# Turning the rows ahead of the FFN by products with a diagonal of the norm's factors, in a two-layer encoder trunk

## The chip, the cores and the metric

The kernel runs on one core of a Trainium2 chip. The metric is the device time of one execution in microseconds; the median of three runs of the kernel before is 2181.53 us (2178.12 to 2184.14). Everything is computed in float32: a product of full accuracy is made either of three products of operands rounded to a shorter type (`fp32r`: high by high, high by low, low by high) or, in a few places, of one plain float32 product.

## The reference, cut to what matters

Two layers work on x of 1024 tokens by 1024 features. Layer 0 mixes by attention, layer 1 by a gated linear recurrence; each ends with a SwiGLU FFN. Every sub-layer is wrapped in two norms:

```python
def rmsnorm(x, g):
    xf = x.astype(jnp.float32)
    y = xf * lax.rsqrt(jnp.mean(xf * xf, axis=-1, keepdims=True) + RMS_EPS)
    return (y * g.astype(jnp.float32)).astype(x.dtype)

# per layer
x = x + rmsnorm(m, norm_mix_post[layer])          # m: the mixer's output
h = rmsnorm(x, norm_ffn_pre[layer])
f = swiglu(h, ffn_w_gate[layer], ffn_w_up[layer], ffn_w_down[layer])
x = x + rmsnorm(f, norm_ffn_post[layer])
```

The change concerns the norm `rmsnorm(x, norm_ffn_pre)`. Its gain vector is multiplied into the FFN's weights, so what is left to do on the rows is the factor per token, 1/sqrt(mean square + eps).

## The kernel before, in words

**Where it happens.** `out_product` computes the mixer's output product (1024 x 1024 by 1024 x 1024) in three passes over the eight token tiles of 128: tiles 0, 1, 2, then 3, 4, 5, then 6 and 7. The product of a tile lands in PSUM (`ps`), and from there it goes through a chain that is the same for every tile t:

1. `rstd`: ScalarE squares `ps` and sums the rows (L179), GpSimd adds eps and takes the power -1/2 (L183, L184).
2. VectorE multiplies `ps` with the gain of the post norm into `mg` (L251), then adds the old x: `x = mg * rs + x` (L257). A DMA stores x (L259).
3. `pre_norm`: `rstd` again, on x (L179, L183, L184), with `mg` as a place for the squares that nobody reads. ScalarE then writes the scaled rows x * rs into `mg` (L213).
4. `turn`: TensorE turns the eight 128 x 128 blocks of `mg` with transposes against the identity (L223) into two PSUM banks `pst`.
5. `HiddenS.take`: ScalarE copies the two banks back into `mg` (L85), VectorE forms differences `tf` (L89) for a Strassen product, ScalarE rounds the pieces into `hS` (L96) and VectorE forms the remainders (L89, also into `hS`).

`hS` is the moving operand of the FFN's gate and up products (`strassen`, L759 to L761).

**What sets the order.** A scheduler with its own estimates of durations puts the instructions of each engine into one fixed list; every engine then works through its list in order, waiting on semaphores. Some orders are written by hand with `behind`: the turns of tiles 3, 4 and 5 stand between the plain float32 products of tile 6 (`raw` by `act`, L602), and the turn of tile 6 stands behind the first of the seven FFN products that use the first 256 columns of `hS` (tiles 0 to 3). The weights of the FFN's first block are prepared in the same stretch (`gate_load`: L717, L729, L730, L736 to L743).

**Buffers.** `mg` has 3, `pst` has 2 banks (tag `tr`), and a turn fills both. x has 2 buffers (tag `nx`), except for tiles 2 and 5, which use a place of their own; the loads of x for tiles 3, 4, 6 and 7 therefore wait until an earlier tile's x is no longer read.

The same stretch occurs twice, at 438 to 600 us (layer 0) and at 1430 to 1570 us (layer 1) of the profiled span. `pre_norm` is also used behind the first FFN (`HiddenT`, 8 tiles, 64 transposes); the change leaves that use as it is.

Of the kernel before, what the change touches and what calls it, by code (L numbers as in the profile page):

```python
# [11 lines left out]
AF = mybir.ActivationFunctionType  # L12
# [3 lines left out]
P = 128  # L16
# [83 lines left out]
class Trunk:  # L100
# [106 lines left out]
    def pre_norm(self, pool, x, h, g, sink, t, psum, later=False):  # L207


        nc = self.nc  # L210
        rs = self.rstd(pool, [x], h)
        if g is None:
            self.scaled = nc.scalar.activation(h, x, AF.Copy, scale=rs).ins  # L213
        else:
            self.scaled = nc.vector.scalar_tensor_tensor(h, x, rs, g, op0=ALU.mult, op1=ALU.mult).ins

        def turn():
            pst = []
            for q in range(2):
                ps = psum()  # L220
                for j in range(4):
                    kt = 4 * q + j
                    self.turned[t] = nc.tensor.transpose(  # L223
                        ps[:, j * P:(j + 1) * P], h[:, kt * P:(kt + 1) * P], self.ident).ins
                pst.append(ps.rearrange("p (a b) -> p a b", a=4))
            return lambda: sink.take(t, pst, h, pool)

        if later:
            return turn
        turn()()  # L230
# [342 lines left out]
    def psum(self):  # L573
        return self.pp.tile([P, 512], F32, tag="mm", bufs=6, name=self.uid("ps"))
# [712 lines left out]
```

## Time and profile before

| | |
|---|---|
| median of 3 runs | 2181.53 us (2178.12 to 2184.14) |
| the profiled execution, its own time | 2188.6 us |
| its span, first to last instruction | 2186.8 us |
| TensorE busy | 2158.0 us, 99% of the span |
| VectorE, ScalarE, GpSimd busy | 1500.0, 1173.2, 220.4 us |
| mean granted TensorE clock | 0.996 |

In the profile, PE is TensorE's matmul side and PEld its loading of stationary operands; DVE is VectorE, ACT ScalarE, POOL GpSimd, SP the queue that issues most DMAs. A row of the timeline gives the start, the time until the result is written (matmuls overlap, so the distance from one start to the next is what one costs), engine, line, operation, tiles and, in brackets, the idle time ahead of it and what ended it. Rows of equal instructions that follow each other are merged. A row of the groups gives the total busy time, the mean of one in ns, and the idle time just ahead of them. A row of the windows gives the busy time of each engine in a stretch and the mean clock that TensorE was granted there (1.00 is full speed).

### The profile page before, as it was taken

What the parts mean: (1) busy time and instruction counts of PE and PEld (TensorE: products, weight loads), DVE (VectorE), ACT (ScalarE), POOL (GpSimd) and SP (SyncE); (2) the same over time, 40 slices, a digit from 0 to 9 for tenths busy, and PEclk for the clock granted to TensorE, in tenths of its full rate; (3) what the DMA queues carried; (4) which work ended last, traced back from release to release, by engine and by line L of the source; (5) the groups of instructions that cost most, each with busy time, mean ns of one, the idle gap of its engine ahead of it and who ended that gap; (6) DMA issues with size and microseconds to landing.
All of it is one profiled execution on the core that took longest, in us unless ns stands there. A gap on an engine that the chain in (4) does not pass through costs nothing.

```text
span 2186.8 us, 30432 instructions
## 1 busy us (share of the span) xinstructions
PE 2158.0 (99%) x11140; PEld 1803.8 (82%) x11140; DVE 1500.0 (69%) x2458; ACT 1173.2 (54%) x2174; POOL 220.4 (10%) x398
## 2 busy tenths in 40 slices
PE   9999999999999999999999999999999999999998
PEld 8888989878788888888887777887788888888886
DVE  5747555656877677767778667437786767758675
ACT  7656555556755445433446576537755454424452
POOL 2111113121100000000002333102100000000011
PEclk9999999999999999999999999999999999999999
DMA  7111012126334233336467311356133333328565
GB/s 284 44 49 49 30 40 64 43 99 205 133 103 133 92 118 99 106 106 242 136 196 225 98 49 54 95 199 230 63 130 102 121 97 98 110 87 293 169 183 154
DMA packets 167453, 269.42 MB, mean 123 GB/s; under 512 B 13964, under 2 KB 94860, under 8 KB 167304
## 3 DMA queue, kind: packets, MB, share of 16 engines
q1 hardware_dynamic: 166520, 265.38, 37.9%
q10 hardware_dynamic: 784, 2.10, 0.3%
q8 instruction: 87, 1.43, 0.3%
q14 instruction: 62, 0.51, 0.1%
HBM read 199.80 MB, written 65.54 MB: 121 GB/s over the span
## 4 chain that ended last, share of the span: by engine, by line
PE 86%; DVE 5%; ACT 3%; DMA 2%; issue 2%; POOL 1%; SPq 0%; POOLq 0%; DVEq 0%; ACTq 0%
PE ps L760 13%; PE ps L759 13%; PE ps L761 13%; PE ps L602 6%; PE ps L845 5%; PE ps L846 5%; PE ps L844 5%; PE pso L370 3%; PE tr L435 3%; PE psq L167 3%; PE psq L168 2%; PE psq L169 2%; PE ps L168 2%; PE ps L169 2%; PE ps L167 2%
## 5 line engine op out<-in xcount | busy, mean ns | idle before, releaser
L759 PE MATMUL ps<-hS,q 128*128 128x512 f32 (+1 forms) x1288 | 490.4, 381 | 0.0
L760 PE MATMUL ps<-hS,q 128*128 128x512 f32 (+1 forms) x1288 | 489.9, 381 | 0.5 <-DVE hS L89 0.5
L761 PE MATMUL ps<-hS,q 128*128 128x512 f32 (+1 forms) x1288 | 489.2, 380 | 0.0
L730 DVE TENSOR_TENSOR q<-raw,q 128x512 fp32r<-128x512 f32 x308 | 205.6, 688 | 180.7 <-ACT q L729 180.1
L760 PEld LDWEIGHTS ps<-hS,q 128*128 128x128 f32 x1288 | 243.1, 189 | 47.0 <-DVE hS L89 0.9
L761 PEld LDWEIGHTS ps<-hS,q 128*128 128x128 f32 x1288 | 243.0, 189 | 46.1
L759 PEld LDWEIGHTS ps<-hS,q 128*128 128x128 f32 x1288 | 242.7, 189 | 46.1 <-DVE tf L89 0.2
L729 ACT CAST q<-raw 128x512 fp32r<-128x512 f32 x308 | 178.8, 619 | 165.4 <-DVE raw L738 127.6
L845 PE MATMUL ps<-o,o 128*128 128x512 f32 x616 | 240.2, 390 | 0.5 <-DVE o L840 0.4
L846 PE MATMUL ps<-o,o 128*128 128x512 f32 x616 | 237.7, 389 | 0.0
L717 ACT ACTIVATE raw<-raw,gcol 128x256 f32<-128x256 f32 x352 | 150.8, 502 | 138.7 <-DMA raw<-in_ffn_w_up_dram 74.8
L844 PE MATMUL ps<-o,o 128*128 128x512 f32 x616 | 218.6, 390 | 1.8 <-ACT o L839 1.8
L839 ACT CAST o<-raw 128x512 fp32r<-128x512 f32 x173 | 104.2, 622 | 148.3 <-PE ps L846 52.5
L183 POOL TENSOR_SCALAR rs<-ss 128x1 f32<-128x1 f32 x52 | 34.0, 654 | 1416.2 <-ACT junk L179 1344.1
L840 DVE TENSOR_TENSOR o<-raw,o 128x512 fp32r<-128x512 f32 x173 | 116.1, 688 | 53.1 <-ACT o L839 52.6
L844 PEld LDWEIGHTS ps<-o,o 128*128 128x128 f32 x616 | 115.3, 188 | 27.2 <-ACT o L839 3.7
L845 PEld LDWEIGHTS ps<-o,o 128*128 128x128 f32 x616 | 115.6, 188 | 25.6 <-DVE o L840 1.8
L846 PEld LDWEIGHTS ps<-o,o 128*128 128x128 f32 x616 | 115.6, 188 | 24.0
L157 DVE TENSOR_TENSOR wlo<-raw,whi 128x1024 fp32r<-128x1024 f32 x76 | 93.4, 1229 | 58.6 <-ACT whi L156 57.3
L423 DVE TENSOR_TENSOR_SCAN pr<-pr,zero 128x128 f32<-128x128 f32 (+7 forms) x64 | 86.6, 1359 | 51.3 <-POOL pr L420 49.6
L156 ACT CAST whi<-raw 128x1024 fp32r<-128x1024 f32 x76 | 79.8, 1052 | 52.1 <-PE ps L168 23.4
L167 PE MATMUL psq<-hT,whi 128*128 128x512 f32 x256 | 102.4, 400 | 1.2 <-ACT v L310 1.0
(208 smaller groups left out, 4278.6 us busy)
## 6 DMA issues: line engine op xcount, KB each, us to landing
raw<-in_ffn_w_gate_dram SPq DMA_DIRECT2D x44, 512.0 KB, 4.2
raw<-in_ffn_w_up_dram SPq DMA_DIRECT2D x44, 512.0 KB, 4.2
gS<-c SPq DMA_DIRECT2D x88, 256.0 KB, 3.8
raw<-gS SPq DMA_DIRECT2D x88, 256.0 KB, 2.8
gA<-c SPq DMA_DIRECT2D x66, 256.0 KB, 3.4
raw<-gA SPq DMA_DIRECT2D x44, 256.0 KB, 2.7
t<-in_ffn_w_down_dram SPq DMA_DIRECT2D x22, 512.0 KB, 6.5
raw<-in_ffn_w_down_dram SPq DMA_DIRECT2D x41, 256.0 KB, 4.8
```

What stands on the lines that cost most here:

```text
L167: nc.tensor.matmul(ps, wh[:, kt, cols], hh[:, kt, :], start=kt == 0, stop=False)
L602: self.matmul = nc.tensor.matmul(ps[:, n * 512:(n + 1) * 512], x, y[:, n, :], start=first and i == 0, stop=last and i == len(passes) - 1).ins
L717: nc.scalar.activation(raw[:, i], raw[:, i], AF.Copy, scale=gain[:, 4 * k + i:4 * k + i + 1])
L729: self.last = nc.scalar.copy(t[:, 0], src).ins
L730: self.last_lo = nc.vector.tensor_tensor(t[:, 1], src, t[:, 0].bitcast(F32), op=ALU.subtract).ins
L759: nc.tensor.matmul(ps, a[:, 0, kt, :], bh, start=kt == 0, stop=False)
L760: nc.tensor.matmul(ps, a[:, 0, kt, :], bl, start=False, stop=False)
L761: self.matmul = nc.tensor.matmul(ps, a[:, 1, kt, :], bh, start=False, stop=kt == 3).ins
L840: tt(t[:, 1], src, t[:, 0].bitcast(F32), op=ALU.subtract)
L844: nc.tensor.matmul(ps, a[0], b[:, 0], start=first, stop=False)
L845: nc.tensor.matmul(ps, a[0], b[:, 1], start=False, stop=False)
L846: self.matmul = nc.tensor.matmul(ps, a[1], b[:, 0], start=False, stop=last).ins
```

## The change

Where the receiver is `HiddenS` (the norms ahead of both FFNs, 16 tiles in all), `pre_norm` no longer writes the scaled rows. ScalarE writes a 128 x 128 diagonal matrix instead: the identity, each row scaled with that token's factor, into a part of `mg`. Step 4 is then no transpose of scaled rows but a plain float32 product of x's block (stationary) with that diagonal (moving), which turns the block and scales it at once. Steps 1, 2, 3's squares, and 5 stay.

```diff
         rs = self.rstd(pool, [x], h)
-        if g is None:
+        scaling = isinstance(sink, HiddenS)
+        if scaling:
+            diag = h[:, 512:512 + P]
+            self.scaled = nc.scalar.activation(diag, self.ident, AF.Copy, scale=rs).ins
+        elif g is None:
             self.scaled = nc.scalar.activation(h, x, AF.Copy, scale=rs).ins
...
                 for j in range(4):
                     kt = 4 * q + j
-                    self.turned[t] = nc.tensor.transpose(
-                        ps[:, j * P:(j + 1) * P], h[:, kt * P:(kt + 1) * P], self.ident).ins
+                    o, c = ps[:, j * P:(j + 1) * P], slice(kt * P, (kt + 1) * P)
+                    self.turned[t] = (nc.tensor.matmul(o, x[:, c], diag, start=True, stop=True) if scaling else
+                                      nc.tensor.transpose(o, h[:, c], self.ident)).ins
```

The scheduler's lists change with it. In the changed kernel the lines behind the edit stand 4 or 5 further down: L213 is L215 (the diagonal), L223 is L228, L251 is L256, L257 is L262, L602 is L607, L612 is L617; L85, L89, L96, L156 and L179 keep their numbers. In the rows below a buffer's number belongs to the built program: `ps_5878`, `ps_5879`, `ps_5880` are the products of tiles 3, 4 and 5 of layer 0, and `pst_5806` with `pst_5811` the two banks of tile 0's turn.

TensorE in layer 0, in the second pass, around the turn of tile 0. Before:

```order
L602 MATMUL ps_5879<-whi_5947,al_5944 128x512
L602 MATMUL ps_5880<-whi_5887,ah_5883 128x512
...
L602 MATMUL ps_5880<-whi_5917,al_5914 128x512
L602 MATMUL ps_5880<-whi_5947,ah_5943 128x512
L223 MATMUL pst_5806<-ident,mg_5768 128x128 x4
L223 MATMUL pst_5811<-ident,mg_5768 128x128 x4
L602 MATMUL ps_5880<-wlo_5948,ah_5943 128x512
```

and now:

```order
L607 MATMUL ps_5879<-whi_5947,al_5944 128x512
L228 MATMUL pst_5806<-mg_5768,x_5769 128x128 x4
L228 MATMUL pst_5811<-mg_5768,x_5769 128x128 x4
L607 MATMUL ps_5880<-whi_5887,ah_5883 128x512
L607 MATMUL ps_5880<-wlo_5888,ah_5883 128x512
L607 MATMUL ps_5880<-whi_5887,al_5884 128x512
```

Tile 0's turn stands 13 products of tile 5 further ahead; the turns of tiles 1 and 2 move ahead likewise, to about where those of tiles 0 and 1 stood.

ScalarE in layer 0, after tile 1's x has been squared (`mg_5778,ss_5832`). `ah_5973`, `whi_6007`, `ah_6003`, `whi_6037` are the rounded operands of the next steps of the second pass. Before:

```order
L213 ACTIVATE mg_5768<-x_5769,rs_5790 128x1024
L213 ACTIVATE mg_5778<-x_5779,rs_5831 128x1024
L179 ACTIVATE mg_5796,ss_5863<-x_5797 128x1024
L612 CAST ah_5973<-act_5971 128x384
L156 CAST whi_6007<-raw_6005 128x1024
L213 ACTIVATE mg_5796<-x_5797,rs_5862 128x1024
L612 CAST ah_6003<-act_6001 128x384
L156 CAST whi_6037<-raw_6035 128x1024
L85 COPY mg_5768<-pst_5806 128x512
L85 COPY mg_5768<-pst_5811 128x512
```

and now:

```order
L215 ACTIVATE mg_5768<-ident,rs_5790 128x128
L215 ACTIVATE mg_5778<-ident,rs_5831 128x128
L179 ACTIVATE mg_5796,ss_5863<-x_5797 128x1024
L85 COPY mg_5768<-pst_5806 128x512
L215 ACTIVATE mg_5796<-ident,rs_5862 128x128
L85 COPY mg_5768<-pst_5811 128x512
L96 CAST hS_5513<-mg_5768 128x8x64
L96 CAST hS_5515<-mg_5768 128x4x64
L617 CAST ah_5973<-act_5971 128x384
L156 CAST whi_6007<-raw_6005 128x1024
```

The copies of tile 0's turned banks, and two roundings behind them, now stand ahead of the operands `ah_5973` and `whi_6007`.

VectorE in layer 0, where tile 6's product `ps_6257` becomes `mg_6355` and then `x_6356` (`tf_6215` belongs to tile 4, `tf_6246` to tile 5, `q` and `raw` to the FFN's weights). Before:

```order
L89 TENSOR_TENSOR tf_6215<-tf_6215,mg_6131 128x256
L251 TENSOR_TENSOR mg_6355<-ps_6257,g_5766 128x1024
L89 TENSOR_TENSOR hS_5518<-tf_6215,hS_5517 128x16x64
L257 SCALAR_TENSOR_TENSOR x_6356<-mg_6355,rs_6359,x_6356 128x1024
L743 TENSOR_TENSOR raw_6387<-raw_6387,raw_6381 128x4x128
```

and now:

```order
L89 TENSOR_TENSOR tf_6215<-tf_6215,mg_6131 128x256
L89 TENSOR_TENSOR hS_5518<-tf_6215,hS_5517 128x16x64
L256 TENSOR_TENSOR mg_6355<-ps_6257,g_5766 128x1024
L89 TENSOR_TENSOR tf_6246<-mg_6162 128x256 x2
L262 SCALAR_TENSOR_TENSOR x_6356<-mg_6355,rs_6359,x_6356 128x1024
L735 TENSOR_TENSOR q_6397<-raw_6381,q_6397 128x512
```

Tile 4's 1024-wide remainder stands ahead of `mg_6355` instead of behind it, and two 256-wide differences of tile 5 stand between `mg_6355` and `x_6356`. Layer 1 has the same three moves. On the SP queue the loads of x for tiles 4 and 5 stand a few issues further back and the store of tile 5's x stands ahead of the loads for tiles 6 and 7; GpSimd's list is the same.

## The prediction

> **What bounds the kernel now.** I read the page's busy times and its chain first.
>
> ```profile
> PE 2158.0 (99%) x11140; PEld 1803.8 (82%) x11140; DVE 1500.0 (69%) x2458; ACT 1173.2 (54%) x2174; POOL 220.4 (10%) x398
> PE 86%; DVE 5%; ACT 3%; DMA 2%; issue 2%; POOL 1%; SPq 0%; POOLq 0%; DVEq 0%; ACTq 0%
> ```
>
> TensorE is busy for 99% of the span and carries 86% of the chain that ended last: work added to it is paid in full, unless it falls into one of its few waits; work taken from ScalarE is worth only what TensorE waits for ScalarE. So the next views are the stretch around the changed norms (layer 0's, as windows) and TensorE's own waits.
>
> ```profile
> 482.00:520.00 38.00, 38.00 (x176) 31.16 (x173) 20.79 (x21) 19.96 (x30) 6.14 (x10) 1.00 0.63 205
> ...
> 545.00:573.00 28.00, 28.00 (x110) 18.14 (x109) 27.31 (x45) 24.84 (x46) 7.24 (x13) 1.00 0.55 202
> 573.00:580.00 7.00, 4.84 (x28) 4.63 (x28) 5.15 (x7) 5.56 (x9) 2.94 (x4) 0.76 0.70 225
> ```
> ```profile
> engine line waited for: us in total, times, longest us
> PE pst L223 <- ACT mg L213: 5.0, 2, 2.8
> PE pst L223 <- ACT mg L85: 1.8, 1, 1.8
> ```
>
> In each window the first pair is PE's busy time. In the first two it has no gap at all; VectorE joins it from 545 on (27.31 of 28.00). Only at 573 to 580 does TensorE stand still (4.84 of 7.00), with the clock down (0.76). In both layers together TensorE waits 5.0 us for the scaled rows, twice, and 1.8 us for the copies of a turned bank, once. That, and what the waits do to the clock, is all that a faster scaling could win.
>
> **The change part by part. First, what a turn costs TensorE.**
>
> ```profile
> L435 PE MATMUL tr<-ident,pr 128*128 128x128 f32 x528 | 83.2, 278 | 0.1
> ...
> L370 PE MATMUL pso<-pt,v 128*64 128x128 f32 x1056 | 66.6, 276 | 1.5 <-ACT pt L441 1.4
> ...
> L602 PE MATMUL ps<-raw,act 128*128 128x512 f32 x64 | 28.5, 592 | 0.0
> ...
> L223 PE MATMUL pst<-ident,mg 128*128 128x128 f32 x128 | 18.7, 290 | 6.8 <-ACT mg L213 5.0 <-ACT mg L85 1.8
> ```
>
> Count the records. A transpose leaves one (L223: 16 tiles x 8 = 128). A plain float32 product leaves two: `raw` by `act` is 2 tiles x 4 steps x 2 halves x 2 layers = 32 products and 64 records, and attention's L370 has 1056 for the 528 blocks that L435 turns one by one. So each of the 128 changed turns becomes two passes. What one costs is the distance between starts:
>
> ```profile
> 520.96 0.39 PE L602 MATMUL ps<-whi,ah 128*128 128x512 f32 x1
> 521.19 1.03 PE L223 MATMUL pst<-ident,mg 128*128 128x128 f32 x8
> 521.98 0.48 PE L602 MATMUL ps<-wlo,ah 128*128 128x512 f32 x1
> 522.29 0.40 PE L602 MATMUL ps<-whi,al 128*128 128x512 f32 x1
> ...
> 557.23 1.88 PE L602 MATMUL ps<-raw,act 128*128 128x512 f32 x4
> 558.95 1.04 PE L223 MATMUL pst<-ident,mg 128*128 128x128 f32 x8
> ```
>
> Eight transposes and the next product take 522.29 - 521.19 = 1.10 us; less the product's 0.23 (520.96 to 521.19) that is 0.87, or 0.109 each. A float32 pass of 512 columns takes (558.95 - 557.23)/4 = 0.43, so 0.108 for 128 columns. Both say 0.109 per pass, 0.218 per product, +0.87 us per tile, and over 16 tiles **+13.9 us**. Bounds for the price of a pass: L370's passes follow at 0.058 (40 in 2.33 us of the chain below), but use half the columns of the array, so that two of them may overlap; at 0.058 the change adds 16 x (16 x 0.058 - 0.87) = +0.9 us. If a pass could not hide its own weight load it would take 0.108 + 0.14 and the change add 49 us; both full-size rows hide it. I take 0.109, the row of the same shape.
>
> ```profile
> 85.11 2.33 PE pso L370 x40
> ```
> ```profile
> L223 PEld LDWEIGHTS pst<-ident,mg 128*128 128x128 f32 x128 | 15.8, 148 | 11.3 <-ACT mg L213 5.4 <-ACT mg L85 3.4 <-issue 1.1
> ```
>
> The Trainium skill's page "TensorE: Matmul & The Clock Gate", Terms, calls the transpose mode four times faster for FP32. By that rule a product costs 4 x 0.109 and the change adds 16 x 8 x 3 x 0.109 = 41.8 us; the two records of each plain product speak for two times, not four.
>
> **Second, ScalarE.** A 128 x 1024 scaling becomes a 128 x 128 one:
>
> ```profile
> L213 ACT ACTIVATE mg<-x,rs 128x1024 f32<-128x1024 f32 x16 | 18.4, 1152 | 10.4 <-POOL rs L184 10.2
> ...
> L415 ACT ACTIVATE pr<-pr,mn 128x128 f32<-128x128 f32 x8 | 3.2, 398 | 2.0 <-DVE mn L407 2.0
> ```
>
> 1.15 us falls to about 0.40 (L415, from SBUF to SBUF and of the same shape), so each tile is ready 0.75 us earlier. For 13 of 16 tiles nobody waits and this is worth nothing. The other three:
>
> ```profile
> 576.47 1.97 PE L223 MATMUL pst<-ident,mg 128*128 128x128 f32 x8 [2.16 <-ACT mg L213]
> ...
> 579.91 0.28 PE L761 MATMUL ps<-hS,q 128*128 128x256 f32 x1
> 580.03 0.28 PE L759 MATMUL ps<-hS,q 128*128 128x256 f32 x1
> ...
> 1526.94 1.14 PE L223 MATMUL pst<-ident,mg 128*128 128x128 f32 x8 [1.77 <-ACT mg L85]
> ...
> 1545.47 1.69 PE L223 MATMUL pst<-ident,mg 128*128 128x128 f32 x8 [2.83 <-ACT mg L213]
> ...
> 1549.40 0.28 PE L759 MATMUL ps<-hS,q 128*128 128x256 f32 x1
> ```
>
> Tile 4 of layer 1 waits 1.77 us for the copies of tile 3's bank, which stand behind tile 4's scaling on ScalarE. They come 0.75 earlier, and TensorE, with tile 3's turn doubled, arrives 0.87 later: 1.77 - 0.75 - 0.87 leaves 0.15. **-1.6 us.**
>
> Tile 6 waits 2.16 and 2.83 us. The doubled turns of tiles 3 to 5 don't shorten this by themselves, since tile 6's product stands behind them too and starts the chain later. The scaling gives 0.75. VectorE's new order gives a little more: a 1.22 us remainder stood between `mg` and x, now two 256-wide differences stand there.
>
> ```profile
> 568.34 1.22 DVE L89 TENSOR_TENSOR hS<-tf,hS 128x1024 fp32r<-128x1024 f32 x1
> ...
> 571.87 0.76 DVE L89 TENSOR_TENSOR tf<-mg 128x256 f32<-128x256 f32 x2
> ...
> 574.42 1.22 DVE L251 TENSOR_TENSOR mg<-ps,g 128x1024 f32<-128x1024 f32 x1
> ```
>
> That is 1.22 - 0.76 = 0.46 at most, none if the remainder now delays `mg` by as much; I take 0.35. Bounds for each wait: a gain of 0.4 to all of it. **-2.2 us** for both; 1.05 and 1.7 us of waiting stay.
>
> The clock is the third thing that a shorter wait moves.
>
> ```profile
> 577.00:578.00 1.00, 1.00 (x6) 1.00 (x5) 0.86 (x2) 0.94 (x2) 0.00 (x0) 0.50 0.55 189
> ...
> 1527.00:1528.00 1.00, 1.00 (x9) 0.94 (x10) 1.00 (x4) 1.00 (x2) 0.00 (x0) 1.00 0.79 320
> ```
>
> After the 2.16 us wait TensorE runs at half clock (0.50); after the 1.77 us one it does not (1.00). From 576.47 to 580.03 pass 3.56 us for 8 transposes and 9 products that at 0.87, 0.12 each (579.91 to 580.03) and 0.08 of switching (522.29 - 521.98 - 0.23) need 2.0; from 1545.47 to 1549.40 it is 3.93 for 8 and 12, which need 2.4. So half clock costs 1.5 us a layer. I count it as gone in layer 0 and as half gone in layer 1, whose 1.7 lies near the 1.77: **-2.25 us** (bounds 0 and -3.0). The Trainium skill's page "TensorE: Matmul & The Clock Gate", Part 1, has the half rate begin after at least one idle window of about 3.4 us; by that rule neither remaining wait would trip it, and the sum would be 0.75 lower, but 2.16 us sufficed in this trace.
>
> **Third, what is moved.** The turns of tiles 0 to 2 move ahead, tile 0's by 13 products of 0.23, from 521.19 to about 518.2. ScalarE is the risk: two copies, a diagonal and two roundings now stand ahead of the second pass's next operands.
>
> ```profile
> 515.73 1.16 ACT L213 ACTIVATE mg<-x,rs 128x1024 f32<-128x1024 f32 x1
> ...
> 520.84 0.50 ACT L612 CAST ah<-act 128x384 fp32r<-128x384 f32 x1
> ...
> 1526.31 1.06 ACT L85 COPY mg<-pst 128x512 f32<-128x512 f32 x2
> ...
> 1528.32 0.92 ACT L96 CAST hS<-mg 128x512 fp32r<-128x512 f32 x2
> ```
> ```profile
> 523.21 0.39 PE L602 MATMUL ps<-whi,ah 128*128 128x512 f32 x1
> ```
>
> Tile 0's factor is there by 515.73, so its turn at 518.2 waits for nothing. The cast of 520.84 moves by up to 1.06 + 0.92 + 0.40 and ends near 523.7. TensorE used it at 523.21, but now reaches that place after 0.87 more for tile 0's turn and 1.74 for tile 1's, near 525.8: covered by 2.1 us, and without that cover it costs what it is late. The loads of x that now wait for a turn instead of a scaling (L195; SP issues the stores and the next weights behind them) are read only at the end of the next pass: free.
>
> Sum: 13.9 - 1.6 - 2.2 - 2.25 = +7.85, say **+8 us**. The profiled execution takes 2188.6 us (a span of 2186.8 and 1.8 around it), so it would take about 2196.5. It stands 7.1 above the runs' median, which moves by the same amount to **2189.5 us**, 0.36% slower.
>
> **The rivals.**
>
> *All of it lands.* The 13.9 us are paid and the waits stay: VectorE, busy 27.31 of 28.00, and not ScalarE's scaling, sets tile 6's chain, and the casts behind the copies cost TensorE a microsecond or two. For it: VectorE's share. Against: tile 6's wait ends with L213 by name. +13 to +15, 2195.5.
>
> *The factor comes early* (not slower). In tile 6's chain GpSimd needs 2.56 us for an addition that takes 0.22 for tile 7:
>
> ```profile
> 572.02 2.56 POOL L183 TENSOR_SCALAR rs<-ss 128x1 f32<-128x1 f32 x1 [3.89 <-ACT mg L179]
> ...
> 580.20 0.22 POOL L183 TENSOR_SCALAR rs<-ss 128x1 f32<-128x1 f32 x1 [4.00 <-ACT mg L179]
> ```
>
> It ends just when VectorE's run of operations from SBUF to SBUF ends (at 574.42, where L251 reads PSUM). In the new order VectorE may pause earlier. Then the diagonal is 2.3 us earlier on top, both waits and both spells of half clock go: 13.9 - 1.6 - 2.16 - 2.83 - 3.0 = +4.3, 2185.8, within what can't be told from no change. It decides once the absorbed part exceeds 7.4 us. Against it: the addition still stands behind x, with 3 us of such operations listed behind it.
>
> *Passes at 0.058.* Then +0.9 on TensorE and a shorter wait at tile 4 by the scaling alone: 0.9 - 0.75 - 2.2 - 2.25 = -4.3, 2177; with the factor early too 0.9 - 0.75 - 2.16 - 2.83 - 3.0 = -7.8, 2173.7. Against it: the transposes, of the same shape, take 0.109.
>
> *Transposes four times faster*, as four passes of 0.109 would have it: 2181.5 + 41.8 - 6 (the three terms above) = 2217. Against it: the record counts.
>
> That the change doesn't do what it says is out: all 16 turns stand as products of x in TensorE's list.
>
> **How the numbers follow.** A difference below 0.3% (6.5 us) can't be told from no change. The forecast has 0.56, its own range +5 to +11, of which 0.16 lies below 6.5; all lands 0.17; the factor early 0.20; cheap passes 0.05 (0.03 faster, 0.02 same); fourfold 0.02. Slower: 0.40 + 0.17 + 0.02 = 0.59; same: 0.16 + 0.20 + 0.02 = 0.38; faster 0.03. The range runs from 2183.5 (the factor early, and a little of the runs' scatter) to 2197 (all lands).
>
> **What would show it.** 256 records of L228 at a distance of 0.109, a turn of 1.74 us; L215 near 0.40; no wait at tile 4 of layer 1; waits of about 1 and 1.7 us at tile 6, with the windows' clock behind them; L183's time for tile 6. It is wrong if a pass takes another time, if TensorE waits in the second pass, or if the waits at tile 6 are gone or as long as before.

## The result, and the profile after

The changed kernel takes 2194.61 us (median of 4 executions, 2192.23 to 2196.42), the kernel before 2181.78 us beside it (median of 4, 2178.12 to 2184.14). The ratio is 1.0061, with an interval of 1.0048 to 1.0074: **13.3 us slower**, 10.5 to 16.1. (Differences from the kernel before are worked out from the ratio here and below; the two medians differ by 12.8.) One later execution of the kernel before, of 3426.93 us at a mean clock of 0.588, is left out of every comparison. The prediction said slower, and its range of 2183.5 to 2197 holds the time. But its own sum was +8; what came is the size that it gave to the rival "all of it lands" (+13 to +15).

The page of the changed kernel, busy times and chain:

```profile
PE 2166.6 (99%) x11268; PEld 1814.4 (83%) x11268; DVE 1498.8 (68%) x2458; ACT 1163.1 (53%) x2174; POOL 211.9 (10%) x398
...
PE 88%; DVE 5%; ACT 3%; DMA 2%; issue 1%; POOL 1%; SPq 0%; POOLq 0%; DVEq 0%; ACTq 0%
```

TensorE has 128 instructions more (11268 against 11140) and carries 88% of the chain in place of 86%. ScalarE is busy 10 us less. The groups of the changed kernel, with their shapes:

```profile
L228 PE MATMUL pst<-mg,x 128*128 128x128 f32 x256 | 31.3, 276 | 2.3 <-ACT mg L215 2.3
...
L215 ACT ACTIVATE mg<-ident,rs 128x128 f32<-128x128 f32 x16 | 6.4, 402 | 13.3 <-POOL rs L184 13.2
```

256 records, two for each of the 128 turns, and a diagonal of 0.402 us: both as forecast. What a turn costs is read from the timeline of the changed kernel, TensorE alone:

```profile
559.69 1.88 PE L607 MATMUL ps<-raw,act 128*128 128x512 f32 x4
561.40 1.95 PE L228 MATMUL pst<-mg,x 128*128 128x128 f32 x16
563.18 1.88 PE L607 MATMUL ps<-raw,act 128*128 128x512 f32 x4
```

From 561.40 to 563.18 are 1.78 us for 16 passes, 0.111 each, where the turn before took 0.87. Each of the 16 turns costs 0.91 us more at most.

TensorE's waits in the changed kernel, and the clock at the three places where the profile shown before had it at half speed (us, busy times, and behind POOL's the granted clock):

```profile
engine line waited for: us in total, times, longest us
PE ps L849 <- ACT o L844: 2.5, 2, 1.7
PE pst L228 <- ACT mg L215: 2.3, 2, 1.3
```
```profile
444.00:450.00 6.00, 4.31 (x26) 3.69 (x26) 4.70 (x21) 4.09 (x13) 2.63 (x4) 1.00 0.81 314
575.00:581.00 6.00, 4.73 (x28) 3.34 (x27) 5.00 (x9) 4.39 (x8) 3.24 (x4) 1.00 0.64 191
1544.00:1550.00 6.00, 4.96 (x22) 2.84 (x20) 5.99 (x10) 3.96 (x8) 2.78 (x4) 1.00 0.51 170
```

Tile 6 waits 1.27 and 1.04 us (2.3 together), tile 4 not at all, and the clock is full. So the savings of the forecast are there when these two profiles are compared, and yet the measured difference is that of the passes alone. The same windows of the kernel before, in the profile shown ahead of the prediction:

```profile
444.00:450.00 6.00, 4.67 (x19) 3.89 (x20) 3.96 (x18) 4.27 (x13) 3.13 (x5) 0.73 0.64 246
575.00:581.00 6.00, 4.53 (x26) 4.53 (x27) 3.57 (x5) 5.39 (x9) 1.74 (x5) 0.72 0.55 186
1544.00:1550.00 6.00, 4.53 (x26) 4.53 (x27) 3.55 (x5) 5.46 (x10) 1.82 (x5) 0.72 0.54 184
```

The profiled executions themselves differ by 4.5 us only (2193.09 and 2188.6). A mean of 0.72 over 6 us is a stretch of some 3.4 us at half speed, a loss of 6 x 0.28 = 1.7 us, three times; the first one, at 446, lies where attention's last products meet the first of the output product, ahead of everything that was changed. The profiled execution of the kernel before stood 7 us above the median. The question for the runs was whether what the change removes is a part of that excess, and so is missing from the other executions.

### The profile page after: what moved, and what is told of

The parts are those of the page before. It is cut to its first block, busy times and chain, and to the rows that moved or that the text cites. A ratio compares the mean times of both kernels' runs of the same rounds, so it can differ in the third digit from the quotient of the medians.

```text
span 2191.3 us, 30702 instructions
## 1 busy us (share of the span) xinstructions
PE 2166.6 (99%) x11268; PEld 1814.4 (83%) x11268; DVE 1498.8 (68%) x2458; ACT 1163.1 (53%) x2174; POOL 211.9 (10%) x398
## 3 DMA queue, kind: packets, MB, share of 16 engines
q8 instruction: 88, 1.44, 0.3%
## 4 chain that ended last, share of the span: by engine, by line
PE 88%; DVE 5%; ACT 3%; DMA 2%; issue 1%; POOL 1%; SPq 0%; POOLq 0%; DVEq 0%; ACTq 0%
PE ps L766 13%; PE ps L765 13%; PE ps L764 13%; PE ps L607 7%; PE ps L849 5%; PE ps L850 5%; PE ps L851 5%; PE pso L375 3%; PE tr L440 3%; PE psq L167 3%; PE psq L168 2%; PE psq L169 2%; PE ps L168 2%; PE ps L167 2%; PE ps L169 2%
## 5 line engine op out<-in xcount | busy, mean ns | idle before, releaser
L764 PE MATMUL ps<-hS,q 128*128 128x512 f32 (+1 forms) x1288 | 489.0, 381 | 0.0
L735 DVE TENSOR_TENSOR q<-raw,q 128x512 fp32r<-128x512 f32 x308 | 205.0, 686 | 181.4 <-ACT q L734 181.2
L764 PEld LDWEIGHTS ps<-hS,q 128*128 128x128 f32 x1288 | 241.6, 188 | 46.1 <-issue 0.5
L849 PE MATMUL ps<-o,o 128*128 128x512 f32 x616 | 218.5, 390 | 2.6 <-ACT o L844 2.5
L844 ACT CAST o<-raw 128x512 fp32r<-128x512 f32 x173 | 103.9, 620 | 149.3 <-PE ps L851 49.5
L183 POOL TENSOR_SCALAR rs<-ss 128x1 f32<-128x1 f32 x52 | 29.8, 572 | 1425.0 <-ACT junk L179 1354.3
L849 PEld LDWEIGHTS ps<-o,o 128*128 128x128 f32 x616 | 115.3, 188 | 28.1 <-ACT o L844 4.3
L156 ACT CAST whi<-raw 128x1024 fp32r<-128x1024 f32 x76 | 79.7, 1050 | 50.4 <-PE ps L168 23.4
```

The costliest lines, as they stand in the source:

```text
L735: self.last_lo = nc.vector.tensor_tensor(t[:, 1], src, t[:, 0].bitcast(F32), op=ALU.subtract).ins
L764: nc.tensor.matmul(ps, a[:, 0, kt, :], bh, start=kt == 0, stop=False)
L849: nc.tensor.matmul(ps, a[0], b[:, 0], start=first, stop=False)
```

## The experiments

The runs of one group ran on the same chip beside the kernel before, whose median was 2179.44 us in the first group (e1 to e4), 2180.30 in the second (e5 to e8) and 2181.46 in the third (e9, e10).

### The kernel before, once more

No edit.

> The kernel before once more, to see the granted clock of its ordinary executions. Theory 1 (the waits of the profile shown before are typical): most executions have the mean clock of that profile, 0.996, that is two or three spells of half clock behind waits, and a span near 2187 us. Theory 2 (the profiled execution was an unlucky one): most executions have 0.998 to 0.999, at most one spell, and 2178 to 2184 us. Ratio 1.000 by both.

2178.93 us (2177.56 to 2183.38, 12 executions), and the profiled one took 2178.35 with a span of 2176.6. That is theory 2, an unlucky first profile. TensorE's waits in it, and tile 6's turn in both layers:

```profile
PE pst L223 <- ACT mg L213: 1.8, 2, 0.9
```
```profile
573.86 1.09 PE L223 MATMUL pst<-ident,mg 128*128 128x128 f32 x8 [0.88 <-ACT mg L213]
...
1536.77 1.09 PE L223 MATMUL pst<-ident,mg 128*128 128x128 f32 x8 [0.88 <-ACT mg L213]
```

Tile 6 waits 0.88 us in place of 2.16 and 2.83; there is no wait at tile 4; and the same three windows show no half speed:

```profile
444.00:450.00 6.00, 4.38 (x25) 3.84 (x26) 4.57 (x20) 4.26 (x14) 2.84 (x4) 1.00 0.71 277
575.00:581.00 6.00, 6.00 (x53) 6.00 (x52) 5.11 (x11) 5.06 (x9) 1.03 (x2) 1.00 0.40 147
1544.00:1550.00 6.00, 5.77 (x49) 5.57 (x48) 4.96 (x12) 2.98 (x6) 0.00 (x0) 1.00 0.01 3
```

That explains the 10.2 us between the two spans (2186.8 and 2176.6) of the same program: 1.77 at tile 4, 4.99 - 1.76 = 3.2 at tile 6, and three half-speed stretches of 1.7, together 10.1. The reason for tile 6's part is GpSimd's first operation on its factor, here 0.35 us long, there 2.56 (572.02 in the prediction's row):

```profile
570.69 0.35 POOL L183 TENSOR_SCALAR rs<-ss 128x1 f32<-128x1 f32 x1 [3.89 <-ACT mg L179]
571.12 0.60 POOL L184 TENSOR_TENSOR rs<-rs,neghalf 128x1 f32<-128x1 f32 x1
```

The prediction's rival "the factor comes early" was thus the ordinary state of the kernel before, not something that the change could bring.

### The same, a third time

No edit.

> The kernel before, unchanged, once more. Theory 1 (the first profile of it showed an uncommon execution): tile 6's factor starts after 0.2 to 0.7 us of GpSimd in both layers, TensorE waits about 0.9 us there twice and not at tile 4, the span is 2176 to 2180 us, with at most one stretch at half the clock ahead of the end. Theory 2 (the slow factor is about as common as the quick one): 2.56 us of GpSimd, waits of over 2 us, span above 2183 us. Ratio 1.000 with either.

2181.52 us (2178.19 to 2185.51, 10 executions), ratio 1.0001 (0.9991 to 1.0010), span 2183.0. The quick factor holds (0.35 us in both layers, waits of 0.92 and 0.88). The rest of the expectation missed: there is a wait of 1.81 us at tile 4, this time in layer 0, and two half-speed stretches:

```profile
PE pst L223 <- ACT mg L85: 1.8, 1, 1.8
```
```profile
444.00:450.00 6.00, 4.72 (x19) 3.90 (x20) 3.92 (x18) 3.43 (x13) 3.18 (x5) 0.72 0.65 249
1181.00:1187.00 6.00, 4.74 (x14) 3.74 (x15) 5.95 (x12) 6.00 (x12) 0.79 (x2) 0.72 1.06 286
```

Tile 4's wait comes from GpSimd too. Its first operation on tile 3's factor took 2.96 us in the two layers where tile 4 then waited (at 1515.18 in the first profile, at 549.06 here), and 0.67 or 0.68 us in the other four layers of the three profiles. In the changed kernel's first profile it took 2.96 us once, in layer 0, and no wait followed:

```profile
549.06 2.96 POOL L183 TENSOR_SCALAR rs<-ss 128x1 f32<-128x1 f32 x1 [2.76 <-ACT mg L179]
```
```profile
550.72 2.96 POOL L183 TENSOR_SCALAR rs<-ss 128x1 f32<-128x1 f32 x1 [2.76 <-ACT mg L179]
```

The first row is of this profile, the second of the changed kernel's.

So the long wait at tile 6 was uncommon (one profile of three, and 2188.6 us is above all those compared later, 2185.51 at most), while tile 4's wait and the half-speed stretches come and go. Those scatter the times over 2177 to 2186 us.

For the stretches there is more than three profiles to go by, since the mean granted clock of every execution is on record. In the profiled executions it was 0.999 where the profile shows no half-speed stretch inside the work, 0.998 with one, 0.997 with two, and 0.996 in the first profile with its three. Of the 84 executions of the kernel before in the three groups, 24 had 0.999, 50 had 0.998, 10 had 0.997 and none 0.996; of the eight of the changed kernel 4, 3 and 1. An ordinary execution thus has none to two, with the change as without it.

### The doubled passes alone

The rows are scaled as before; only the transposes become plain products with the identity.

```diff
-                    self.turned[t] = nc.tensor.transpose(
-                        ps[:, j * P:(j + 1) * P], h[:, kt * P:(kt + 1) * P], self.ident).ins
+                    o, c = ps[:, j * P:(j + 1) * P], slice(kt * P, (kt + 1) * P)
+                    self.turned[t] = (nc.tensor.matmul(o, h[:, c], self.ident, start=True, stop=True)
+                                      if isinstance(sink, HiddenS) else
+                                      nc.tensor.transpose(o, h[:, c], self.ident)).ins
```

> ScalarE scales the whole rows as before, and only the transposes become plain float32 products, of the scaled rows with the identity. If the doubled passes are the cost (16 turns x 0.87 us), of which only the 1.77 us wait of tile 4 in layer 1 absorbs 0.87: +13 us, ratio 1.006, with the waits at tile 6 as long as before (2 to 3 us). If the cost came from the moved orders on ScalarE and VectorE instead: under +7 us.

2195.27 us (5 executions), ratio 1.0070 (1.0057 to 1.0082), which is +15.3 us. Its turns take 1.78 us as in the changed kernel, and tile 6 waits 1.44 us twice:

```profile
PE pst L224 <- ACT mg L213: 2.9, 2, 1.4
```

So the shorter operation on ScalarE, the whole purpose of the diagonal, is worth the difference between 1.0070 and 1.0061: about 2 us, and as the intervals overlap it may be nothing. In the traces of the two it is 2.9 - 2.3 = 0.6 us at tile 6.

### The shorter scaling alone

Each block of x is turned by a one-pass transpose against the diagonal. The factor's power is set to 0, so that the diagonal is the identity: this kernel leaves out the scaling by the norm's factor. Its operations are otherwise those of the change. The edit is shown against the changed kernel, without the lines that hand the power through.

```diff
-        rs = self.rstd(pool, [x], h)
         scaling = isinstance(sink, HiddenS)
+        rs = self.rstd(pool, [x], h, self.zero if scaling else None)
...
-                    self.turned[t] = (nc.tensor.matmul(o, x[:, c], diag, start=True, stop=True) if scaling else
+                    self.turned[t] = (nc.tensor.transpose(o, x[:, c], diag) if scaling else
                                       nc.tensor.transpose(o, h[:, c], self.ident)).ins
```

> ScalarE builds the 128 x 128 diagonal as in the change, but the turns stay transposes with one pass. The power in these 16 factors is 0 instead of -1/2, so the diagonal is the identity and the scaling of the rows is left out; every operation keeps its size and its place in the chain. Theory 1: what the shorter operation wins alone, 0.75 (tile 4 of layer 1) + 2.2 (tile 6, twice) + 2.25 (half clock) = -5 us. Theory 2: no half clock to win back in ordinary executions, -3 us. If VectorE sets tile 6's chain: 0 to -1 us.

2180.35 us (11 executions), ratio 1.0005 (0.9997 to 1.0014): no gain. The wait at tile 6 is gone, and another took its place, in both layers:

```profile
PE ps L764 <- ACT hS L96: 2.9, 2, 1.4
```
```profile
586.55 1.04 ACT L96 CAST hS<-tf 128x1024 fp32r<-128x1024 f32 x1 [3.29 <-DVE tf L89]
...
587.64 0.74 PE L764 MATMUL ps<-hS,q 128*128 128x256 f32 x4 [1.44 <-ACT hS L96]
```

An FFN product now reaches the last rounded pieces of `hS` before ScalarE has made them, and waits 1.44 us, more than the 0.88 saved ahead of it. Both waits lie in the same short stretch, behind the same chain of VectorE and ScalarE; a head start for the turn alone doesn't shorten that chain.

### The change at tile 6 alone

The diagonal and the products for tile 6 of each layer, the one tile whose turn TensorE waits for in every profile of the kernel before; the other 14 turns as before. The edit is one to the changed kernel.

```diff
-        scaling = isinstance(sink, HiddenS)
+        scaling = isinstance(sink, HiddenS) and t == 6
```

> The diagonal and the plain products for tile 6 of each layer alone; the other 14 tiles as before. Passes +1.7 us; the two waits at tile 6 shorter by 1.1 each. Theory 1: with the half clock gone 1.7 - 2.2 - 2.25 = -2.7 us. Theory 2: -0.5 us. If VectorE sets tile 6's chain: +1.7 us.

2183.03 us (11 executions), ratio 1.0014 (1.0005 to 1.0022), +3 us. Here GpSimd takes 0.35 us, and the diagonal is ready when TensorE arrives:

```profile
571.98 0.35 POOL L183 TENSOR_SCALAR rs<-ss 128x1 f32<-128x1 f32 x1 [3.89 <-ACT mg L179]
...
573.95 0.39 ACT L215 ACTIVATE mg<-ident,rs 128x128 f32<-128x128 f32 x1
...
574.39 2.05 PE L228 MATMUL pst<-mg,x 128*128 128x128 f32 x16
```

The 0.88 us of waiting are gone, so the saving of 0.75 us on ScalarE does what the prediction said. It only pays for the second pass of the same turn (0.91), and a wait of 0.3 us follows in the FFN's products. By its trace that is 0.9 - 0.88 + 0.3, less than half a microsecond a layer, where +3 us were measured (1.1 to 4.8 by the interval). Its profile also has a half-speed stretch at 446, and TensorE waits 5.1 us there for ScalarE at the down product (L849), where the three profiles of the kernel before show 1.8, 2.6 and 4.2: both come and go without any edit. The rest isn't accounted for. Even at the one tile that waits, the change earns nothing.

### The changed kernel without VectorE's weight work beside tile 6's factor

VectorE's last three splits of the gate weights are held behind tile 6's diagonal.

```diff
-                squared, summed = self.squared, self.summed
+                squared, summed, scaled = self.squared, self.summed, self.scaled
...
-        last, products, hold = first([*last_m, summed], psum)
+        last, products, hold = first([*last_m, summed, scaled], psum)
```

In the changed kernel GpSimd's L183 for tile 6 takes 1.89 us again, while VectorE runs its splits of the weights (L735) and a difference (L89). Rows of the changed kernel:

```profile
576.82 1.89 POOL L183 TENSOR_SCALAR rs<-ss 128x1 f32<-128x1 f32 x1 [3.54 <-ACT mg L179]
...
577.00 0.69 DVE L735 TENSOR_TENSOR q<-raw,q 128x512 fp32r<-128x512 f32 x1
...
577.94 0.69 DVE L735 TENSOR_TENSOR q<-raw,q 128x512 fp32r<-128x512 f32 x1
...
578.79 0.57 POOL L184 TENSOR_TENSOR rs<-rs,neghalf 128x1 f32<-128x1 f32 x1
```

> The changed kernel, with one thing more: tile 6's diagonal is put ahead of the last three splits of the gate weights (S3, S1, S4), so that VectorE runs no operation of weights while GpSimd computes tile 6's factor. In the changed kernel GpSimd's first operation on that factor took 1.89 us in both layers and TensorE then waited 1.27 and 1.04 us. Theory 1 (VectorE's run of operations holds GpSimd up, and this is all that makes tile 6 wait): the operation falls to 0.2 to 0.4 us, the wait at tile 6 to under 0.3 us, and the kernel gains about 2 us on the changed one: ratio to before about 1.005. Theory 2 (the lateness is in the operations before the factor): the operation falls or not, the wait stays at about 1 us, ratio 1.006. Theory 3: the splits are late in turn, and the products with S3 wait: no gain, ratio 1.006 or more.

2195.07 us (5 executions), ratio 1.0066 (1.0053 to 1.0078). With the splits moved behind, the same operation takes 0.22 us in both layers and tile 6's wait falls to 0.58:

```profile
577.62 0.22 POOL L183 TENSOR_SCALAR rs<-ss 128x1 f32<-128x1 f32 x1 [3.53 <-ACT mg L179]
577.92 0.57 POOL L184 TENSOR_TENSOR rs<-rs,neghalf 128x1 f32<-128x1 f32 x1
578.73 1.02 ACT L179 ACTIVATE junk<-ps 128x1024 bf16<-128x1024 f32 x1
...
579.74 0.39 ACT L215 ACTIVATE mg<-ident,rs 128x128 f32<-128x128 f32 x1
...
580.18 2.05 PE L228 MATMUL pst<-mg,x 128*128 128x128 f32 x16 [0.58 <-ACT mg L215]
```

That VectorE's work on the weights holds GpSimd up in this order is shown. The Trainium skill's page "SBUF — State Buffer", section "SBUF: two separate sides", says that VectorE and GpSimd share one pair of ports, which one of them holds for a whole instruction while the other blocks, for VectorE operations with two inputs in SBUF among others; 1.89 against 0.22 us fits that. But VectorE's operations beside it take 0.42 to 0.69 us each, so more than one of them kept it out, and it doesn't hold for every execution: in the order of the kernel before, the same neighbours gave 2.56 us in one profile and 0.35 in two.

Of the 1.67 us gained at the factor 0.69 and 0.46 reach TensorE: the factor is there at 578.49, and the diagonal starts at 579.74, since tile 7's squares (L179) stand ahead of it in ScalarE's list. In the time nothing is gained that could be measured: the operation fell as theory 1 had it, the wait and the ratio did not.

### The scaling in two halves

The kernel before, with the scaled rows written in two halves.

```diff
-            self.scaled = nc.scalar.activation(h, x, AF.Copy, scale=rs).ins
+            self.scaled = [nc.scalar.activation(h[:, a:b], x[:, a:b], AF.Copy, scale=rs).ins for a, b in (((0, 512), (512, D)) if isinstance(sink, HiddenS) else ((0, D),))][-1]
```

> The kernel before, with ScalarE's scaling of a tile done in two halves of 512 columns, so that the first four transposes can start after the first half. If tile 6's transposes wait for ScalarE's 1.14 us as such, the wait of 0.88 us per layer falls by about 0.5 us, and the kernel gains up to 1 us: ratio 0.9995. If the scaling is hidden wherever it stands (the theory that the row shortened by the change is worth nothing), ratio 1.000. Rival: the two halves cost ScalarE 0.2 us more per tile and change its order; then a wait appears at another tile and the ratio is 1.0005 or more.

2184.28 us (11 executions), ratio 1.0022 (1.0013 to 1.0031): slower by 4.8 us. The scheduler's lists changed around it, the wait at the turns rose to 1.3 us in its worst place, and a second one came at the FFN's products:

```profile
PE pst L223 <- ACT mg L213: 2.5, 2, 1.3
PE ps L759 <- ACT hS L96: 2.0, 2, 1.1
```

The two halves take 1.34 us where the one operation took 1.15. By this trace the waits are 2.7 us longer than in the kernel before; the rest of the 4.8 isn't accounted for. The rival of that expectation held in the main, though the new wait is one of the FFN's products and not of another tile's turn.

### The factor late on purpose, before and after

Both kernels get five more operations on GpSimd (rs times 1.0) behind tile 6's factor, so that what the first profile had by chance is there in every execution.

```diff
-        rs = self.rstd(pool, [x], h)
+        rs = self.rstd(pool, [x], h); late = [nc.gpsimd.tensor_scalar(rs, rs, 1.0, None, op0=ALU.mult) for _ in range(5 if isinstance(sink, HiddenS) and t == 6 else 0)]
```

> The kernel before, with five more small operations on GpSimd (the factor times 1.0) behind tile 6's factor in each layer, which makes it late by some 1.5 to 2.2 us (such an operation stands 0.35 to 0.43 us before the next one). It puts on purpose what the first profile of the kernel before had by chance. Theory 1 (a wait of over 2 us at tile 6 brings a stretch of 3.4 us at half the clock behind it, which costs 1.7 us): waits of 2.4 to 3.1 us in place of 0.88, a half-clock stretch behind each, and +6 to +8 us on the kernel before: ratio 1.003 to 1.0035. Theory 2 (the half clock comes by chance, whatever the wait): no stretch, +3 to +4.4 us, ratio 1.0015 to 1.002.

> The changed kernel with the same five operations on GpSimd behind tile 6's factor in each layer. Theory 1 (the savings of the forecast are real once the factor is late, since the diagonal takes 0.40 us where the rows took 1.14, and the shorter wait brings less of the half clock): 8 to 10 us over the kernel before with the same delay. Theory 2 (the order of the work around tile 6 takes the saving back, late or not): the waits are as long as in the kernel before with the same delay, within 0.3 us, and it stands 13 to 15 us over it: ratio to the kernel before 1.0085 to 1.010.

The late kernel before takes 2184.25 us (11 executions), ratio 1.0019 (1.0010 to 1.0028); the late changed kernel 2201.99 us (4 executions), ratio 1.0103 (1.0089 to 1.0116). The first, +4 us, is the number of theory 2, but its profile shows a half of theory 1. Both layers wait 2.37 us, and the clock falls behind one of the two waits:

```profile
576.55 1.97 PE L223 MATMUL pst<-ident,mg 128*128 128x128 f32 x8 [2.37 <-ACT mg L213]
...
1543.38 1.09 PE L223 MATMUL pst<-ident,mg 128*128 128x128 f32 x8 [2.37 <-ACT mg L213]
```
```profile
576.00:582.00 6.00, 5.45 (x34) 5.45 (x35) 4.22 (x6) 5.27 (x9) 0.80 (x2) 0.72 0.39 150
...
1543.00:1549.00 6.00, 5.62 (x48) 5.62 (x49) 5.34 (x10) 5.12 (x9) 1.49 (x2) 1.00 0.37 144
```

Eight transposes take 1.97 us in the first row and 1.09 in the second. So a wait of this length may or may not cost the clock. On the average it does: 8 of the 11 late executions have a mean clock of 0.997 and 3 of 0.998, where 2 of the 21 beside them have 0.997 and the others 0.998 or 0.999. The two means, 0.9982 and 0.9973, lie as far apart as one stretch would put them (1.7 of 2180 us is 0.0008), so the two waits bring about one more stretch to an execution.

The medians of the late pair stand 17.7 us apart, more than either theory said. TensorE waits 3.89 us in each layer of the late changed kernel against 2.37, and both waits bring half speed, in layer 0 for twice as long:

```profile
581.40 0.40 ACT L215 ACTIVATE mg<-ident,rs 128x128 f32<-128x128 f32 x1 [2.44 <-POOL rs L211]
...
581.86 3.78 PE L228 MATMUL pst<-mg,x 128*128 128x128 f32 x16 [3.89 <-ACT mg L215]
```
```profile
582.00:588.00 6.00, 6.00 (x30) 6.00 (x31) 2.92 (x6) 2.85 (x6) 0.46 (x2) 0.53 0.21 87
...
1555.00:1561.00 6.00, 3.71 (x19) 3.71 (x20) 2.28 (x3) 1.08 (x3) 2.01 (x6) 0.72 0.47 167
```

From the end of GpSimd's work to the turn it needs less than the other (the diagonal starts at 581.40 and the turn at 581.86, 0.46 us; in the late kernel before 1.20, from 575.35 to 576.55). The 0.74 us are there, then; but the factor itself is later, since GpSimd's L183 takes 1.89 us in this order (0.35 in the other) and tile 4's rounding (L96) stands ahead of tile 6's first square (L179). With the factor late the change doesn't win back its price either.

### The changed kernel, once more

No edit.

> The changed kernel, unchanged, once more. Theory 1 (GpSimd's 1.89 us on tile 6's factor comes with this order of the work): 1.89 us again in both layers, waits of 1.0 to 1.5 us at tile 6, span 2190 to 2194 us, ratio 1.005 to 1.007. Theory 2 (it comes by chance from execution to execution): another duration, between 0.2 and 2.6 us, and the wait with it.

2192.79 us (2191.28 to 2194.80, 4 executions), ratio 1.0057 (1.0042 to 1.0072), span 2189.5. GpSimd's operation takes 1.89 us in both layers, as in the first profile of the changed kernel, in the doubled passes alone and in the late one, and tile 6 waits 1.04 us twice. Theory 1 held. So in this order of the work the 1.89 us are the rule, as 0.35 are in the order before.

### Where the time comes from

Lengths of stretches, from the first TensorE products of the lines that begin them (the output product L602/L607, the first FFN product L759/L764, the down product L844/L849), in us:

| | before, first profile | before, again | changed | doubled passes alone |
|---|---|---|---|---|
| layer 0, output product to FFN (6 turns) | 126.0 | 124.4 | 129.8 | 129.8 |
| layer 0, FFN to down product (2 turns) | 426.6 | 423.7 | 425.5 | 425.7 |
| down product to layer 1's output product | 444.5 | 444.3 | 444.5 | 446.9 |
| layer 1, output product to FFN (6 turns) | 97.2 | 94.9 | 100.4 | 100.4 |
| layer 1, FFN to down product (2 turns) | 427.3 | 423.7 | 425.2 | 425.7 |

Against "before, again", the changed kernel pays 5.4 and 5.5 us for six doubled turns (6 x 0.91 = 5.5), and 1.8 and 1.5 for two (1.8): 14.2 us in all, and the two waits that differ (1.27 and 1.04 for 0.88 twice) are hidden in the scatter. (The 126.0 of the first profile holds the half-speed stretch at 446, the 446.9 of the doubled passes one at 1186.) Against the first profile the same stretches differ by 3.8, -1.1, 3.2 and -2.1.

## Why the prediction was right or wrong

**The passes (+13.9): right.** Two records to a product, 0.111 us each where 0.109 was forecast, every one paid: 16 x 0.91 = 14.6 at most by the timeline, 14.2 by the stretches. The rivals "passes at 0.058" and "transposes four times faster" are out.

**Tile 4 (-1.6): right as a mechanism, wrong as a saving on the median.** The wait is in none of the five profiles with all turns doubled, even where GpSimd was as late as it was in the first profile (2.96 us, once). But the kernel before has it only where GpSimd is late: in layer 1 once, in layer 0 once, and not at all in "before, again".

**Tile 6 (-2.2): the step that failed, together with the next.** Against the profile that it was read from, the term is good (4.99 us of waiting fell to 2.31). In the other two profiles of the kernel before the waits are 1.76 and 1.80 us together, and in the new order they didn't fall but grew, to 2.31 and 2.08. The 0.75 us from ScalarE are real (tile 6 alone, the late pair); GpSimd's 1.89 us and the work that the scheduler put ahead of tile 6's square took them back. VectorE's new order gave what was forecast between `mg` and x: 3.55 us from the start of L251 to the end of L257 before, 3.08 from L256 to L262 now. But `mg` itself comes later behind the product of tile 6: tile 4's remainder, which now stands ahead of it, waits for ScalarE's rounding, and behind that rounding stands tile 6's square (L179, at 571.20) too. Rows of the changed kernel:

```profile
571.33 1.22 DVE L89 TENSOR_TENSOR hS<-tf,hS 128x1024 fp32r<-128x1024 f32 x1 [1.11 <-ACT hS L96]
572.47 1.22 DVE L256 TENSOR_TENSOR mg<-ps,g 128x1024 f32<-128x1024 f32 x1
```

The prediction had this as a bound (nothing is gained "if the remainder now delays `mg` by as much") and took 0.35 all the same.

**The clock (-2.25): failed in the same way.** The three stretches at half speed were of that one execution; most of what the change was to save here is not there ordinarily. The other profiles of the kernel before have none and two, neither of them behind tile 6; the two of the changed kernel have none, its variants up to two, and the mean clocks of all executions say the same. Nor did the length of the wait decide as the prediction had it (2.16 us cost the clock, 1.77 did not): in the same profile the stretch at 446 followed a wait of 1.76 us.

```profile
445.30 0.33 PE L403 MATMUL sc<-st,st 128*128 128x128 f32 x1 [1.76 <-DVE mn L407]
```

**The step from the profile to the median: the error behind both.** The prediction put it thus: the profiled execution "stands 7.1 above the runs' median, which moves by the same amount". That sentence carries the error. The three savings, 6.05 us, were waits and half clock of the execution that was 7.1 us too long, and they are for the most part what made it so. Taken off the median they were saved twice: the median lacked these waits already. Without them the same sum says +13.9, and +13.3 was measured.

**What was moved: right.** In both kernels the second pass has no wait, and the rounded operands stay ahead.

**The rival "all of it lands"** named the size but another cause: that VectorE keeps the waits as they are. VectorE has a part in it, by way of GpSimd's factor, but the waits were short already. The range held because that rival was inside it; the forecast's own range, +5 to +11, doesn't hold the 13.3, so that the stated range did is luck.

## What to carry to other kernels

Before a term is taken from a wait, hold the profiled execution against the median of the runs: when it stands 7 us above, look for what in it is not ordinary (a small operation of 2.56 us that takes 0.22 elsewhere, stretches at half clock), and expect to save little of that. The mean clock of the other executions tells whether the profile's half-speed stretches are ordinary, without another profile. On an engine that is busy 99% of the time, added passes are paid one by one, while a shorter operation elsewhere pays only at a wait that is there in most executions, and often gives it back at the next one in the same chain. A float32 product in place of a float32 transpose costs a second pass, here 0.111 us for 128 columns.

## What the runs showed of the hardware

A half-speed stretch follows a wait only sometimes. Of two waits of 2.37 us in one execution, one was followed by it; soon behind the wait at the end of attention (1.76, 1.89 and 1.65 us) it came in the first and the third of three profiles of the kernel before. A stretch lasted 3.4 us and cost about 1.7; after 3.89 us of waiting it came both times, once for twice as long. The Trainium skill's page "TensorE: Matmul & The Clock Gate", Part 1, describes a window of about 3.4 us that runs freely, regardless of when the work starts, so that the same kernel meets it at another phase each time; that agrees with the scatter, and with the 3.4 us that a stretch lasts, but no run here sets the phase. Its threshold of one idle window does not agree: waits of 1.65, 1.76, 2.16 and 2.37 us were enough.

An operation of GpSimd on 128 x 1 numbers took 0.22 us or up to 2.96. Moving VectorE's work on weights away brought it from 1.89 to 0.22 us. The long ones of the two kernels (1.89, 2.56 and 2.96 us, on the factors of tiles 3 and 6) all ended within 0.2 us of the place where VectorE's run of operations on SBUF gave way to the product with the gain, which reads PSUM (L251, L256). What decides between 0.35 and 2.56, or 0.68 and 2.96, in one and the same order stays open.
